# Attention scores computed once, probabilities transposed, value products by features

## The chip, the cores and the metric

The kernel runs on one core of one Trainium2 chip. The metric is the time of one execution in device microseconds (us). The median of three runs of the kernel before is 2375.67 us (2374.99 to 2377.59).

## The reference, cut to what matters

The program is a block of two mixing layers with a feed-forward part; the change touches one of the mixers of the second layer, causal attention over 1024 tokens with 8 heads of 64 features and a forget gate whose running sum `c` is added to the scores:

```
q = rms_norm(q, q_g); k = rms_norm(k, k_g); c = cumsum(log_f)
logits = einsum('bhqd,bhkd->bhqk', q_i, kt) * 64 ** -0.5 + (c_i[:, None] - ck[None, :])
logits = where(kpos <= qpos, logits, -inf)
p = softmax(logits)
o = einsum('bhqk,bhkd->bhqd', p, vt)
```

The output of attention is multiplied by a gate, `silu(z)`, and goes with the other mixers' outputs through an output matrix of 2048 x 1024.

## The kernel before

All data are float32. A product that has to be precise is split: `qs` and `kd` hold a rounded high part, `kl` and the second half of `qs` the remainders, so that two matmuls give the exact score. Heads are treated in pairs hp = 0 to 3 (a pair is 128 features). The program is written as generators ("streams") that `weave` runs in turn, and a scheduler then fixes the order of each engine's instructions; a stream waits for buffers by `need` and for another stream's result by `after`. The stage of attention is made of these streams:

`att_load` (L2225) loads a pair's queries and keys by token, transposes them on PE (`pqk`), and builds, for each head x, `qs` (features in rows 64x to 64x+63, the remainder in the other 64 rows), `qm` (a copy of the high part in rows 0 to 63, zeros below), `kd` (the keys' high part twice) and `kl` (the keys' remainder in rows 0 to 63, and eight rows of -1).

`att_max` (L2282) computes the scores by query rows, block by block (12 blocks of up to 512 columns for a head: `kd` against `qs`, `kl` against `qm`, and a mask on the diagonal). One DVE instruction for each block adds the forget term and takes the row maximum (L2305). When all eight row blocks are done, the maxima are transposed and written into rows 64 to 71 of `qm` (L2315), where they meet the rows of -1 in `kl`.

`att_head` (L2321) waits for that and computes the scores again, this time by key rows (`pT`, L2351 and L2352, another 12 blocks), so that the maximum is subtracted on the way. ACT takes the exponential from PSUM to SBUF (L2355, `pt`), and `pt` is the stationary operand of the value products (L2335): 128 queries by 96 columns of `va`, which has 65 columns for each head, the last of them ones, so that the sum of a row comes with its output. The outputs are divided by it on DVE (L2366, L2367).

`att_out` (L2373) transposes the outputs of a pair back to features, multiplies them by the gate and stores them. `mix_loads` and `final` then read the stored mixer outputs and the output weights; `final` starts when all four pairs are stored, and takes all eight PSUM banks.

Two heads run side by side ("m" and "M", "h" and "H" in `STREAMS2`), and `project2`'s last gates (`pz`) are still computed on PE when the first pair begins. DMA issues are mostly on SyncE (SP), in one queue.

Of the kernel before, what the change touches and what calls it, by code (L numbers as in the profile page):

```python
# [30 lines left out]
STREAMS2 = "sknpl013mM2hH564fx7"  # L31
# [44 lines left out]
def tile_block(ctx: ExitStack, tc: tile.TileContext, A, out):  # L76
# [650 lines left out]
    vau = []  # L727
# [1269 lines left out]
    v_dram = dr.tile([SEQ, 520], F32, name="vd")  # L1997
# [4 lines left out]
    def qkv(q):  # L2002
        yield from after(f"u{q}")
        for j in range(3):
# [10 lines left out]
            if j == 2:  # L2015
                for t in range(4):
                    r0 = (4 * q + t) * 128
                    x = yield from spare("vst", (128, 8, 65), order=("ub", "u"))
                    g.memset(x[:, :, 64:65], 1.0)
                    s.activation(x[:, :, 0:64], p[t][:].rearrange("p (h d) -> p h d", d=64), AF.Copy)  # L2020
                    nc.scalar.dma_start(v_dram[r0:r0 + 128, :], x[:].rearrange("p h d -> p (h d)"))
                    free(x, p[t])
# [202 lines left out]
    def att_load(hp):  # L2225
        if hp == 0:
            yield from after("lru", "sn1")
        yield from need(u=8, ub=2)
        va = ub("vau")
        g.memset(va[:, 1040:1072], 0.0)  # L2230
        nc.sync.dma_start(va[:, 0:1040].rearrange("p (c f) -> p c f", c=8),
                          v_dram[:].rearrange("(c p) f -> p c f", p=128)[:, :, hp * 130:hp * 130 + 130])
        oat = ub("oat", (128, 8, 128))
        for x in range(2):
            heads[2 * hp + x] = dict(qs=u("qs", dt=F32R), qm=u("qm", dt=F32R), kd=u("kd", dt=F32R),
                                     kl=u("kl", dt=F32R), va=va, oat=oat)
            H = heads[2 * hp + x]
# [15 lines left out]
        for hf in range(2):  # L2253
            for j in range(2):
# [9 lines left out]
                for x in range(2):  # L2264
# [3 lines left out]
                    if j == 0:  # L2268
# [13 lines left out]
    def att_max(h):  # L2282
        yield from after(f"pair{h // 2}")
        H = heads[h]
        qs, qm, kd, kl = (H[n] for n in ("qs", "qm", "kd", "kl"))
# [5 lines left out]
        for ib in range(8):  # L2291
            tk = slice(ib * 128, (ib + 1) * 128)
            n = (ib + 1) * 128
            for j0 in range(0, n, 512):
                w = min(512, n - j0)
                yield from need(ps=1, f=1)
                p = bank("pS2")
                diag = j0 + w == n
                wc = max(w, 256)
                pe.matmul(p[:, 0:wc], qs[:, tk], kd[:, j0:j0 + wc], start=True, stop=False)  # L2300
                pe.matmul(p[:, 0:wc], qm[:, tk], kl[:, j0:j0 + wc], start=False, stop=not diag)
                if diag:
                    pe.matmul(p[:, w - 128:w], identb[:], mask[1][:], start=False, stop=True)
                junk = f512("junk")
                v.tensor_tensor_reduce(junk[:, 0:w], p[:, 0:w], nb[:, j0:j0 + w], 1.0, -3e38, op0=ALU.add,  # L2305
                                       op1=ALU.max, accum_out=mx[:, j0 // 512, ib:ib + 1])
                free(p, junk)
                yield 0.45, 0.0
        free(nb)
        v.tensor_tensor(mx[:, 0], mx[:, 0], mx[:, 1], op=ALU.max)  # L2310
        yield 0.0, 2.0
        yield from need(ps=1)
        p = bank("pmr")
        pe.transpose(p[0:8, 0:128], mx[:, 0, :], ident[:])
        v.tensor_tensor(qm[64:72].rearrange("p (c t) -> p c t", c=8), p[0:8, 0:128].unsqueeze(1).to_broadcast([8, 8, 128]),  # L2315
                        ident[0:8, 0:8].unsqueeze(2).to_broadcast([8, 8, 128]), op=ALU.mult)
        free(p)
        done.add(f"max{h}")
        yield 0.1, 1.5

    def att_head(h):  # L2321
        yield from after(f"max{h}")
        H = heads[h]
        qs, qm, kd, kl = (H[n] for n in ("qs", "qm", "kd", "kl"))
        for hf in range(2):
            nj = 4 * (hf + 1)
            yield from need(ps=1)
            pO = bank("pO", (128, 4, 96))
            pe.matmul(pO[:], onesb[:], zerob[:, 0:96].unsqueeze(1).to_broadcast([128, 4, 96]),
                      start=True, stop=False)  # L2330

            def values_(jb, x):
                for b in range(max(0, jb - 4 * hf), 4):
                    o = 130 * jb + 65 * (h % 2)
                    pe.matmul(pO[:, b, :], x[:, jb % 2, b * 128:(b + 1) * 128], H["va"][:, o:o + 96],  # L2335
                              start=False, stop=jb == nj - 1 and b == 3)
                if jb % 2:
                    free(x)

            prev = None  # L2340
            for jb in range(nj):
                i0 = max(0, jb * 128 - hf * 512)
                tk = slice(jb * 128, (jb + 1) * 128)
                if jb % 2 == 0:
                    pt = yield from spare("pt", (128, 2, 512), order=("u", "ub"))
# [253 lines left out]
```

## Time and profile before

| | |
|---|---|
| median of 3 runs | 2375.67 us |
| the profiled execution | 2377.7 us, its span 2376.0 us |
| TensorE (PE) busy | 2240.9 us (94%) |
| VectorE (DVE) busy | 1196.1 us (50%) |
| ScalarE (ACT) busy | 794.1 us (33%) |
| GpSimd (POOL) busy | 941.3 us (40%) |
| stage of attention | 1986.6 to 2189.0 us of the span |

PE's durations are those of a pipeline: one matmul begins before the last has ended, so the rate of PE is read from the distances of starts. Weight loads (PEld) run beside matmuls. A matmul of plain float32 operands is issued as two instructions; one of rounded operands, and a transpose, as one.

### The profile page before, as it was taken

How to read it: one execution, taken by the hardware profiler on the slowest of the kernel's cores; microseconds unless marked ns; L12 is line 12 of the kernel's file. 1: busy time of each engine (PE TensorE's matmuls, PEld its weight loads, DVE VectorE, ACT ScalarE, POOL GpSimd, SP SyncE). 2: the span in 40 equal slices, each digit the busy share in tenths (PEclk: the TensorE clock that was granted, in tenths of full speed). 3: DMA queues.
4: the chain of work that ended last, by engine and by line, in shares of the span. 5: the costliest groups of instructions: out<-in, count | busy, mean ns of one | idle time of the engine just before them, and what ended most of it. 6: DMA issues, size and time to landing. Idle time of an engine off the chain costs nothing.

```text
span 2376.0 us, 29812 instructions
## 1 busy us (share of the span) xinstructions
PE 2240.9 (94%) x11022; PEld 1782.9 (75%) x11022; DVE 1196.1 (50%) x2120; ACT 794.1 (33%) x1417; POOL 941.3 (40%) x846
## 2 busy tenths in 40 slices
PE   5998889797999999999999998999999999999998
PEld 2787657575678888888888876787777777778877
DVE  7689744886871212121121686665545675662011
ACT  2423222433342121111112255343333354543322
POOL 4465534747553222232324534123653133120543
PEclk7999989799999999999999999999999999999999
DMA  7211444344222111111121244243575434231564
GB/s 272 96 48 54 139 151 151 120 150 142 84 82 70 45 49 43 56 49 47 42 62 62 93 142 154 74 155 109 167 211 165 169 111 138 67 116 65 156 192 142
DMA packets 161202, 263.82 MB, mean 111 GB/s; under 512 B 16216, under 2 KB 67224, under 8 KB 161056
## 3 DMA queue, kind: packets, MB, share of 16 engines
q1 hardware_dynamic: 126672, 217.12, 29.0%
q10 hardware_dynamic: 32112, 37.02, 4.7%
q0 software_dynamic: 2272, 7.77, 0.9%
q8 instruction: 87, 1.43, 0.3%
q14 instruction: 59, 0.48, 0.1%
HBM read 208.06 MB, written 52.74 MB: 110 GB/s over the span
## 4 chain that ended last, share of the span: by engine, by line
PE 64%; DVE 16%; DMA 7%; issue 4%; POOL 4%; ACT 3%; SPq 1%; ACTq 0%; POOLq 0%; DVEq 0%
PE pf L253 6%; PE pf L255 6%; PE pf L251 6%; PE pz L251 5%; PE pz L253 5%; PE pz L255 5%; PE pg L238 3%; PE pg L239 3%; PE pg L240 3%; PE pO L2335 2%; DVE cv L809 2%; PE pfo L238 2%; PE pfo L239 2%; PE pfo L240 2%; POOL wlo L212 1%
## 5 line engine op out<-in xcount | busy, mean ns | idle before, releaser
L212 POOL TENSOR_TENSOR wlo<-raw,whi 128x512 fp32r<-128x512 f32 (+1 forms) x285 | 397.7, 1397 | 847.0 <-ACT whi L215 828.2
L215 ACT ACTIVATE whi<-raw 128x512 fp32r<-128x512 f32 (+1 forms) x432 | 267.2, 622 | 984.7 <-PE pf L253 291.7
L212 DVE TENSOR_TENSOR wlo<-raw,whi 128x512 fp32r<-128x512 f32 (+1 forms) x147 | 111.6, 759 | 368.3 <-ACT whi L215 367.8
L255 PE MATMUL pf<-h,wlo 128*128 128x512 f32 x704 | 231.8, 392 | 2.8 <-DVE wlo L212 1.9
L251 PE MATMUL pf<-h,whi 128*128 128x512 f32 x704 | 231.9, 392 | 0.1
L253 PE MATMUL pf<-h,whi 128*128 128x512 f32 x704 | 231.8, 392 | 0.0
L251 PE MATMUL pz<-u,whi 128*128 128x512 f32 x512 | 171.9, 403 | 0.9 <-DVE sptmp L1794 0.6
L253 PE MATMUL pz<-u,whi 128*128 128x512 f32 x512 | 167.6, 395 | 0.0
L255 PE MATMUL pz<-u,wlo 128*128 128x512 f32 x512 | 167.5, 395 | 0.0
L255 PEld LDWEIGHTS pf<-h,wlo 128*128 128x128 f32 x704 | 132.3, 188 | 33.2 <-DVE wlo L212 2.4
L251 PEld LDWEIGHTS pf<-h,whi 128*128 128x128 f32 x704 | 132.5, 188 | 29.6 <-ACT whi L215 0.5
L253 PEld LDWEIGHTS pf<-h,whi 128*128 128x128 f32 x704 | 132.5, 188 | 29.4
L239 PE MATMUL pg<-wlo,act 128*128 128x512 f32 x352 | 138.3, 393 | 0.7 <-DVE wlo L212 0.6
L238 PE MATMUL pg<-whi,act 128*128 128x512 f32 x352 | 137.2, 393 | 1.4 <-ACT whi L215 1.4
L240 PE MATMUL pg<-whi,act 128*128 128x512 f32 x352 | 137.0, 392 | 0.0
L251 PEld LDWEIGHTS pz<-u,whi 128*128 128x128 f32 x512 | 95.9, 188 | 25.2 <-issue 2.6
L253 PEld LDWEIGHTS pz<-u,whi 128*128 128x128 f32 x512 | 96.3, 188 | 22.8 <-issue 1.4
L255 PEld LDWEIGHTS pz<-u,wlo 128*128 128x128 f32 x512 | 95.9, 188 | 22.4 <-issue 1.2
L1579 DVE TENSOR_TENSOR x<-x,pg 128x512 f32<-128x512 f32 x80 | 53.6, 685 | 109.1 <-PE pg L240 108.9
L239 PE MATMUL pfo<-wlo,mix 128*128 128x512 f32 x256 | 100.4, 393 | 1.0 <-POOL wlo L212 0.9
L240 PE MATMUL pfo<-whi,mix 128*128 128x512 f32 x256 | 100.2, 393 | 0.0
L1552 DVE TENSOR_TENSOR a<-a,pf 128x512 f32<-128x512 f32 x44 | 28.6, 683 | 141.0 <-PE pf L255 140.9
(638 smaller groups left out, 4902.3 us busy)
## 6 DMA issues: line engine op xcount, KB each, us to landing
raw<-in_w_ffn_in_dram SPq DMA_DIRECT2D x108, 256.0 KB
wm<-in_w_mod_dram SPq DMA_DIRECT2D x48, 512.0 KB
raw<-in_w_out_dram SPq DMA_DIRECT2D x96, 256.0 KB
raw<-in_w2f_dram SPq DMA_DIRECT2D x66, 256.0 KB
raw<-in_w_ffn_out_dram SPq DMA_DIRECT2D x56, 256.0 KB
raw<-in_w2q_dram SPq DMA_DIRECT2D x48, 256.0 KB
raw<-in_w_in_dram SPq DMA_DIRECT2D x36, 256.0 KB
mraw<-y2d SPq DMA_DIRECT2D x32, 256.0 KB
```

Source lines behind the costliest of these rows:

```text
L212: (v if dve else g).tensor_tensor(lo, full, hi, op=ALU.subtract)
L215: s.activation(hi, full, AF.Copy)
L238: pe.matmul(p, lh, rh, start=start, stop=False)
L239: pe.matmul(p, lh, rl, start=False, stop=False)
L240: pe.matmul(p, ll, rh, start=False, stop=stop)
L251: pe.matmul(p, wh, xh[k], start=k == 0, stop=False)
L253: pe.matmul(p, wh, xl[k], start=False, stop=False)
L255: pe.matmul(p, wl, xh[k], start=False, stop=k == kt - 1)
L809: v.scalar_tensor_tensor(a3, *tap(k), a3, op0=ALU.mult, op1=ALU.add)
L1552: v.tensor_tensor(a_[:], a_[:], pair[1][hf][:], op=ALU.mult)
L1579: v.tensor_tensor(x, x, p[t][:], op=ALU.add)
L2335: pe.matmul(pO[:, b, :], x[:, jb % 2, b * 128:(b + 1) * 128], H["va"][:, o:o + 96], start=False, stop=jb == nj - 1 and b == 3)
```

## The change

The scores are computed once, by query rows (`att_rows`). The DVE instruction keeps the sums of scores and forget term in SBUF (`pr`) as it takes the maximum; `anm` is the negated maximum of a row block, and ACT takes the exponential of a whole row block in place, from SBUF to SBUF, and adds it up in the same instruction (`ell`). PE transposes the probabilities, 128 x 128 at a time, into PSUM, from where DVE and ACT in turn copy them to `pt`. In the value products (`att_values`) 64 columns of `va` are now the stationary operand and the transposed probabilities the moving one, 128 columns; the two heads of a pair write the two halves of the partitions of `pO`, so that the output comes by features and isn't transposed. The gate is multiplied in from `pO`; the reciprocal sums of a pair are transposed (`plr`), written to DRAM, read back spread over partitions (`rb`), and multiplied in by POOL. A head's rows may run two row blocks ahead of its values, and a pair's rows begin when the values of six row blocks of the pair before are written out.

`kl` now holds the keys' remainder in the rows in which `qs` holds the queries' high part, and zeros in the others, so that `qs` serves for both score matmuls; `qm` is gone, and with it the rows for the maxima. `va` has 64 columns for each head. There are three streams in place of four, and values stand ahead of rows in `STREAMS2`.

```diff
-STREAMS2 = "sknpl013mM2hH564fx7"
+STREAMS2 = "sknpl013hmM2564fx7"
...
-                    x = yield from spare("vst", (128, 8, 65), order=("ub", "u"))
-                    g.memset(x[:, :, 64:65], 1.0)
-                    s.activation(x[:, :, 0:64], p[t][:].rearrange("p (h d) -> p h d", d=64), AF.Copy)
+                    x = yield from spare("vst", (128, 512), order=("ub", "u"))
+                    s.activation(x[:], p[t][:], AF.Copy)
...
-        yield from need(u=8, ub=2)
+        if hp > 1:
+            yield from after(f"val{hp - 2}")
+        yield from need(u=8, ub=1)
...
-            g.memset(_r(H["kl"][64:128, :]), 0.0)
-            g.memset(_r(H["kl"][64:72, :]), -1.0)
-            g.memset(_r(H["qm"][64:128, :]), 0.0)
+            g.memset(_r(heads[2 * hp + x]["kl"][64 - 64 * x:128 - 64 * x, :]), 0.0)
...
-                        g.tensor_copy(half(H["qm"], hf)[0:64], _r(half(H["qs"], hf)[r0]))
...
-                        v.scalar_tensor_tensor(half(H["kl"], hf)[0:64], src, col("kg")[r0],
+                        v.scalar_tensor_tensor(half(H["kl"], hf)[r0], src, col("kg")[r0],
...
+    def att_rows(h):
...
+        for ib in range(9):
+            if ib < 8:
+                while ib - ahead.get(hp, 0) > 1 or hp and ahead.get(hp - 1, 0) < 6:
+                    yield 0.0, 0.7
...
+                    pe.matmul(p[:, 0:wc], qs[:, tk], kd[:, j0:j0 + wc], start=True, stop=False)
+                    pe.matmul(p[:, 0:wc], qs[:, tk], kl[:, j0:j0 + wc], start=False, stop=not diag)
+                    if diag:
+                        pe.matmul(p[:, w - 128:w], identb[:], mask[1][:], start=False, stop=True)
+                    v.tensor_tensor_reduce(x[:, j0:j0 + w], p[:, 0:w], nb[:, j0:j0 + w], 1.0, -3e38, op0=ALU.add,
+                                           op1=ALU.max, accum_out=mx[:, j0 // 512, ib:ib + 1])
...
+                nm = small("anm", [128, 1], bufs=4)
+                v.tensor_scalar(nm[:], mx[:, 0, ib:ib + 1], mx[:, 1, ib:ib + 1], -1.0, op0=ALU.max, op1=ALU.mult)
+                s.activation(x[:, 0:n], x[:, 0:n], AF.Exp, bias=nm[:], accum_out=ell[:, hp % 2, h % 2, ib:ib + 1])
...
+                for b0 in range(0, m, 4):
+                    k = min(4, m - b0)
+                    yield from need(ps=1)
+                    p = bank("pP", (128, 4, 128))
+                    for b in range(k):
+                        pe.transpose(p[:, b, :], y[:, (b0 + b) * 128:(b0 + b + 1) * 128], ident[:])
+                    if (m + h) % 2:
+                        s.activation(t[:, b0:b0 + k, :], p[:, 0:k, :], AF.Copy)
+                    else:
+                        v.tensor_copy(t[:, b0:b0 + k, :], p[:, 0:k, :])
...
+    def att_values(hp):
...
+                for jb in range(ib + 1):
+                    for x in range(2):
+                        pe.matmul(pO[64 * x:64 * x + 64, b, :], va[:, jb, 64 * x:64 * x + 64], PT[2 * hp + x, ib][:, jb, :],
+                                  start=jb == 0, stop=jb == ib)
+                free([PT.pop((2 * hp + x, ib)) for x in range(2)])
+                ahead[hp] = ib + 1
...
+            v.scalar_tensor_tensor(zh, zh, 0.5, pO[:].rearrange("p a b -> p (a b)"), op0=ALU.mult, op1=ALU.mult)
...
+        v.reciprocal(le, le)
...
+        pe.transpose(p[0:16, 0:128], le, ident[:])
...
+        v.tensor_copy(lr[:], p[0:16, 0:128])
...
+        nc.sync.dma_start(la_dram[16 * hp:16 * hp + 16, :], lr[:])
...
+            nc.sync.dma_start(rb[64 * x:64 * x + 64], la_dram[16 * hp + 8 * x:16 * hp + 8 * x + 8, :].unsqueeze(0)
+                              .to_broadcast([64, 8, 128]))
...
+        g.tensor_tensor(z[:], z[:], rb[:].rearrange("p a b -> p (a b)"), op=ALU.mult)
```

What stands on PE before, while heads of the first pairs are computed for the second time (`pT` are scores by key rows, `pO` opens a bank by a product with zeros and then takes value products):

```order
L2351 MATMUL pT<-qs,kd 128x256
L2352 MATMUL pT<-qm,kl 128x256
L2354 LDWEIGHTS identb
L2354 MATMUL pT<-mask_81,identb 128x128
L2329 LDWEIGHTS onesb
L2329 MATMUL pO<-zerob,onesb 128x384
L2335 MATMUL pO<-vau,pt 128x96
L2351 MATMUL pT<-qs,kd 128x512
L2352 MATMUL pT<-qm,kl 128x512
L2335 MATMUL pO<-vau,pt 128x96 x6
```

Now PE has, at the end of the first pair (`pP` are transposes of `pr`, `pt_16155` and `pt_16184` the transposed probabilities of its two heads, `pS2_16255` scores of the second pair):

```order
L2359 MATMUL pO_16058<-pt_16184,vau_15505 64x128
L2326 MATMUL pP_16197<-ident_69,pr_16142 128x128 x4
L2326 MATMUL pP_16203<-ident_69,pr_16142 128x128 x4
L2359 MATMUL pO_16058<-pt_16155,vau_15505 64x128
L2359 MATMUL pO_16058<-pt_16184,vau_15505 64x128
L2305 MATMUL pS2_16255<-kd_15855,qs_15854 128x256
L2306 MATMUL pS2_16255<-kl_15856,qs_15854 128x256
L2308 LDWEIGHTS identb_73
L2308 MATMUL pS2_16255<-mask1_86,identb_73 128x128
L2373 MATMUL plr_16260<-ident_69,ell_737 16x128
```

The second pass of scores and the opening of banks are gone; transposes stand among value products, which come head by head in turn, and the next pair's scores begin before the last values of this one.

On DVE before, at the end of the first heads' maxima (`amx` the maxima, `qm` where they are written, `ard` and `oat` the division of outputs):

```order
L2305 ISA amx 128x1
L2310 TENSOR_TENSOR amx<-amx 128x8
L2270 SCALAR_TENSOR_TENSOR qs<-pqk,qg,qs 64x512 x3
L2315 TENSOR_TENSOR qm<-pmr,ident 8x1024
L2270 SCALAR_TENSOR_TENSOR qs<-pqk,qg,qs 64x512
L2366 RECIPROCAL ard<-pO 128x4
L2276 SCALAR_TENSOR_TENSOR kl<-pqk,cols,kd 64x512
L2367 TENSOR_TENSOR oat<-pO,ard 128x4x64
```

Now DVE has, late in the first pair (in brackets the engines for which an instruction waits; ISA is the reduction and the read of its accumulator):

```order
L2330 COPY pt<-pP 128x512 [waits PE_49]
L2309 ISA pr,amx<-pS_16087,negcb 128x384 [waits PE_49]
L2309 ISA amx 128x1
L2314 TENSOR_SCALAR anm<-amx 128x1 [waits DVE_49,Activation_49]
L2314 TENSOR_SCALAR anm<-amx 128x1 [waits DVE_49]
L2365 SCALAR_TENSOR_TENSOR za<-za,pO 128x512 [waits DMAHW3_49,PE_49]
L2309 ISA pr,amx<-pS_16130,negcb 128x512 [waits PE_49]
```

The write of all maxima and the divisions are gone; copies of transposed probabilities and a negation for each row block stand among the reductions, and some negations wait for ACT.

## Rows read from the trace of the kernel before

**Rows 1.** The page's first part: busy time, share, instructions of PE.

```profile
PE 2240.9 (94%) x11022; PEld 1782.9 (75%) x11022; DVE 1196.1 (50%) x2120; ACT 794.1 (33%) x1417; POOL 941.3 (40%) x846
```

**Rows 2.** Stretches: length, busy PE, PEld, DVE, ACT, POOL (instructions), clock, DMA share, GB/s.

```profile
2020.00:2060.00 40.00, 37.04 (x236) 27.99 (x234) 36.31 (x101) 23.03 (x37) 5.91 (x13) 1.00 0.29 86
2060.00:2100.00 40.00, 40.00 (x317) 36.37 (x316) 7.82 (x19) 20.12 (x37) 6.89 (x9) 1.00 0.20 60
2100.00:2140.00 40.00, 36.95 (x235) 28.11 (x235) 34.23 (x107) 16.66 (x27) 8.88 (x8) 1.00 0.37 126
2140.00:2189.00 49.00, 49.00 (x380) 44.52 (x379) 9.14 (x30) 21.83 (x42) 1.27 (x1) 1.00 0.18 55
sum 202.40, PE 193.80 PEld 161.52 DVE 101.84 ACT 94.93 POOL 38.78; mean PE 32.30 PEld 26.92 DVE 16.97 ACT 15.82 POOL 6.46
```

**Rows 3.** The chain of waits from 1986.6 to 2189 us, shares by line.

```profile
by line: PE pO L2335 29.1%; PE pT L2351 8.9%; PE pT L2352 8.2%; DVE junk L2305 6.2%; PE pS L2300 5.4%; PE pS L2301 4.6%; PE pz L251 3.9%; PE pz L253 3.8%; PE pz L255 3.8%; issue 2.8%; DVE qs L2270 2.2%; DVE kl L2276 2.1%; PE pT L2354 2.1%; 
```

**Rows 4.** PE in order of time, 2176 to 2182 us: start, us, what.

```profile
2176.59 3.09 PE L2335 MATMUL pO<-vau,pt 128*128 128x96 f32 x26
2179.47 0.48 PE L2351 MATMUL pT<-qs,kd 128*128 128x512 f32 x1
...
2180.70 0.39 PE L2351 MATMUL pT<-qs,kd 128*128 128x512 f32 x1
2180.93 0.39 PE L2352 MATMUL pT<-qm,kl 128*128 128x512 f32 x1
```

**Rows 5.** PE in order of time around a state-space value product, and its tile.

```profile
1698.93 1.28 PE L1953 MATMUL pyo<-xc,state 128*128 128x128 f32 x10
1700.14 1.97 PE L1966 MATMUL pyd<-lt,xdt 128*64 128x128 f32 x32
1702.04 1.98 PE L1978 MATMUL pst<-xdec,xst 128*128 128x512 f32 x4
...
L1966 PE MATMUL pyd<-lt,xdt x32: 272/273/323, 1700.1 to 1701.8; 128*64 128x128 f32 x32
```

**Rows 6.** PE in order of time, transposes of outputs.

```profile
2187.69 0.93 PE L2384 MATMUL pao<-ident,oat 128*128 128x128 f32 x7
...
2188.46 0.36 PE L2335 MATMUL pO<-vau,pt 128*128 128x96 f32 x2
```

**Rows 7.** Groups on DVE, 1986 to 2189 us: shapes, count, busy us, mean ns, idle.

```profile
L2305 DVE CUSTOM_DVE_ANT_0 junk<-pS,negcb 128x512 f32<-128x512 f32 x48 | 32.0, 686 | 5.1 <-PE pS L2301 2.4 <-DMA za<-zg 1.6 <-DMA negcb<-negcd 0.6
...
L2315 DVE TENSOR_TENSOR qm<-pmr,ident 8x1024 fp32r<-8x1024 f32 x8 | 9.7, 1216 | 4.1 <-PE pmr L2314 4.0
...
L2305 DVE DVE_READ_ACCUMULATOR2_ANT amx<- 128x1 f32 x96 | 7.9, 82 | 0.0
...
L2367 DVE TENSOR_TENSOR oat<-pO,ard 128x256 f32<-128x256 f32 x15 | 6.3, 423 | 0.4
...
L2305 DVE CUSTOM_DVE_ANT_0 junk<-pS,negcb 128x128 f32<-128x128 f32 x16 | 4.6, 287 | 10.7 <-PE pS L2303 10.7
```

**Rows 8.** ACT groups: the first of 1985 to 2200 us, others of the span.

```profile
L2355 ACT ACTIVATE pt<-pT,negc 128x512 f32<-128x512 f32 (+3 forms) x96 | 51.4, 580 | 65.7 <-PE pT L2354 49.0 <-PE pT L2352 12.7 <-DVE amx L2305 1.5
...
L1862 ACT ACTIVATE xst<-ptt 128x512 f32<-128x512 f32 x20 | 11.1, 597 | 4.0 <-PE ptt L1861 4.0
...
L2355 ACT ACTIVATE pt<-pT,negc 128x128 f32<-128x128 f32 x16 | 5.9, 366 | 14.6 <-PE pT L2354 14.5
...
L2112 ACT ACTIVATE ga<-tr,lrun 128x1024 f32<-128x1024 f32 x4 | 5.0, 1248 | 0.1
...
L1659 ACT ACTIVATION_READ_ACCUMULATOR xu<-x 128x1 f32 x8 | 1.5, 184 | 0.0
```

**Rows 9.** Groups on DVE, whole span: a small operation, a PSUM copy.

```profile
L286 DVE TENSOR_SCALAR rs<-rs 128x2 f32<-128x2 f32 x8 | 3.7, 465 | 0.1
...
L455 DVE COPY modrow<-pmod 128x512 f32<-128x512 f32 x4 | 2.7, 686 | 4.5 <-PE pmod L442 4.5
```

**Rows 10.** The chain of waits, 2300 to 2376 us: start, us, what.

```profile
2314.09 3.06 DMA mraw<-y2d
```

More of the change, by code (lines that the diff above doesn't have):

```diff
@@ L2280, in att_load @@
         done.add(f"pair{hp}")
-    def att_max(h):
-        yield from after(f"pair{h // 2}")
+    PT, ahead = {}, {}
+    la_dram = dr.tile([64, 128], F32, name="lad")
+    ell = const.tile([128, 2, 2, 8], F32, name="ell")
+    def att_rows(h):
+        hp = h // 2
+        yield from after(f"pair{hp}")
         H = heads[h]
-        qs, qm, kd, kl = (H[n] for n in ("qs", "qm", "kd", "kl"))
+        qs, kd, kl = (H[n] for n in ("qs", "kd", "kl"))
         nb = yield from spare("negcb", order=("ub", "u"))
@@ L2290, in att_max @@
         yield 0.0, 3.0
[L2291 to L2308, printed above, removed]
@@ L2317, in att_max @@
         free(p)
[L2318 to L2345, printed above, removed]
-                yield from need(ps=1)
-                p = bank("pT")
-                ic = min(i0, 256)
-                i_ = slice(hf * 512 + ic, hf * 512 + 512)
-                diag = jb >= 4 * hf
-                pe.matmul(p[:, ic:512], kd[:, tk], qs[:, i_], start=True, stop=False)
-                pe.matmul(p[:, ic:512], kl[:, tk], qm[:, i_], start=False, stop=not diag)
-                if diag:
-                    pe.matmul(p[:, i0:i0 + 128], identb[:], mask[0][:], start=False, stop=True)
-                s.activation(pt[:, jb % 2, i0:512], p[:, i0:512], AF.Exp, bias=negc[:, h, jb:jb + 1])
-                free(p)
-                yield 0.45, 0.0
-                if prev:
-                    values_(*prev)
-                    yield 0.22 * (4 - max(0, jb - 1 - 4 * hf)), 0.0
-                prev = jb, pt
-            yield 0.0, 1.0
-            values_(*prev)
-            yield 0.22, 0.5
-            rd = small("ard", [128, 4, 1], bufs=4)
-            v.reciprocal(rd[:], pO[:, :, 64:65])
-            v.tensor_tensor(H["oat"][:, 4 * hf:4 * hf + 4, 64 * (h % 2):64 * (h % 2) + 64], pO[:, :, 0:64],
-                            rd[:].to_broadcast([128, 4, 64]), op=ALU.mult)
-            free(pO)
-        free(qs, qm, kd, kl)
-        done.add(f"head{h}")
@@ L2373, in att_out @@
-    def att_out(hp):
-        yield from after(f"head{2 * hp}", f"head{2 * hp + 1}", f"za{hp}")
-        yield from need(u=1)
-        z = u("za")
-        nc.sync.dma_start(z[:], z_dram[f"za{hp}"][:])
-        oat = heads[2 * hp]["oat"]
-        yield 0.0, 3.0
-        for hf in range(2):
-            yield from need(ps=1)
-            p = bank("pao")
-            for c in range(4):
-                pe.transpose(p[:, c * 128:(c + 1) * 128], oat[:, 4 * hf + c, :], ident[:])
-            v.scalar_tensor_tensor(half(z, hf), half(z, hf), 0.5, p[:], op0=ALU.mult, op1=ALU.mult)
-            free(p)
-            yield 0.5, 0.0
-        free(oat, heads[2 * hp]["va"])
+        nc.sync.dma_start(la_dram[16 * hp:16 * hp + 16, :], lr[:])
```

87 lines of the change are left out of this document (68 added, 19 removed).

## Prediction

> **What bounds the kernel now.** I read the page's busy shares first: TensorE (PE) is busy 94% of the span, VectorE (DVE) 50%, ScalarE (ACT) 33% [rows 1]. A share over the whole span says nothing of one stage, so I then asked for a table by stretch of the stage that the change touches, from the first transposes of queries and keys (1986.6 us) to the last value product (2189 us), 202.4 us [rows 2]. The reader is to see two kinds of stretch there. From 2060 to 2100 and from 2140 on PE is busy all the time and DVE has 8 to 9 us of work: these are the score blocks that are computed a second time and the value products. From 2020 to 2060 and from 2100 to 2140 DVE is busy 36.3 and 34.2 us of 40 while PE is at 37: there the row maxima are taken and the next pairs' queries and keys made. The chain of waits over the stage [rows 3] says the same by line: value products 29.1%, the repeated scores (L2351, L2352) 17%, and only about 10% on DVE's lines shown. So PE bounds this stage, and DVE is a close second in a third of it. What follows the stage is 768 output matmuls at 0.23 us each, 177 of the 187 us left; the change does not touch them, so what the stage gains should reach the end.
>
> PE durations on the page overlap, so I take the distance of starts. 26 value products take 2.88 us, 0.111 us each, and a score matmul of 512 columns takes 0.23 us [rows 4]; for 384, 256 and 128 columns I estimate in proportion. A 128x128 transpose takes 0.110 us (seven in 0.77 us) [rows 6].
>
> **The change, part by part.** PE before, at these rates: 576 value instructions (288 products, each issued twice) x 0.111 = 63.9 us; scores, for each head 12 blocks of two matmuls (six of 512 columns, two of 384, four of 256: 4.4 us) and 8 masks at 0.06, 4.9 us, so 39.2 us for eight heads, and that twice, 78.4; 64 transposes of queries and keys 7.0; 32 of outputs 3.5; bank openings and transposed maxima, by the same proportion, about 3.5; the last 96 projection matmuls 22.1. Sum 178 us, in a stage of 202.4: 88%, the rest is waiting and change of operands.
>
> *Scores once.* 39.2 us of PE go, with 96 exponentials on ACT (51.4 us [rows 8]). *The stacked queries instead of a copy.* The low part of the keys meets the same stationary tile as the high part, so no PE work changes; the copies to qm (POOL), two of three clearings and the 1.2 us write of the maxima into qm go (9.7 us of DVE, [rows 7]), and with that write the wait of a head's scores for all its maxima.
>
> *Probabilities transposed.* 288 transposes at 0.110 add 31.7 us to PE. Their 96 evacuations are shared: 48 on DVE, priced by a 512-column PSUM copy of 0.686 and by the 128-column reduction of 0.287 [rows 7, 9], mean size 384 columns, 0.55 us, 26.5 us; 48 on ACT, from 0.597 for 512 columns [rows 8] to about half of that for 128 (an estimate), mean 0.49 us, 23.5 us.
>
> *Value products by features.* The new form, 64 stationary and 128 moving columns with the two heads of a pair in the two column halves, stands in the trace: 32 instructions (16 products) start between 1700.14 and 1701.8, and the next matmul at 1702.04 [rows 5]. Eight pairs take 1.75 us, 0.218 for two products; the old form takes 4 x 0.111 = 0.444. In the new order 131 pairs stand together and 26 products alone; if one alone costs as much as a pair, 157 x 0.218 = 34.2 us in place of 63.9. Going into this form and out again costs something: ten matmuls from 1698.93 at 0.111 would end at 1700.04, the first of the new form comes 0.10 later, and the exit (1701.8 + 0.11 against 1702.04) costs about 0.1 again. The order has 52 visits, so I add 0.2 x 52 = 10.4 us; if the switch is hidden behind a wait, nothing. The Trainium skill, page "TensorEngine Tiling (Array Packing)", section "Key Properties", says that a change of tiling mode drains TensorE, which speaks against small visits; the two gaps above agree. Without the drain the PE sum would be 10 us smaller. No row shows pairs that accumulate over several key blocks; that is a rival below.
>
> PE after: 39.2 + 7.0 + 31.7 + 34.2 + 10.4 + 22.1 = 144.6 us, 33 less. The 96 projection matmuls run while DVE and ACT make the first pair; for each of the four pairs PE has (144.6 - 22.1) / 4 = 30.6 us.
>
> *Exponentials by rows.* 64 on ACT, of 128 to 1024 columns, 0.366 to 1.25 us (the ends are L2355's shortest form and ga's [rows 8]), mean 0.81, 51.7 us, and 64 accumulator reads at 0.184, 11.8 us. 64 negated maxima on DVE: between an accumulator read of 0.082 [rows 7] and a small tensor-scalar of 0.465 [rows 9]; I take 0.2, near the smaller operation, 12.8 us (5 to 30).
>
> DVE in the stage: 101.8 [rows 2] - 9.7 (qm) - 6.3 (oat) + 26.5 + 12.8 = 125 us; without projection and weight work (7 us) 29.6 a pair. ACT: 94.9 - 51.4 + 51.7 + 11.8 + 23.5 = 130.5; without the same other work (12 us) 29.6 a pair. So the three engines come to 30.6, 29.6 and 29.6 us a pair. PE no longer bounds alone: a row block goes from PE (scores) to DVE (maximum), ACT (exponential), PE (transposes), DVE or ACT (copy) and PE (values), and each engine keeps its own order.
>
> How much of the time can three such engines be busy? The rows give one measure: where DVE and PE were both needed, DVE was busy 36.3 of 40 and 34.2 of 40 us, 88% [rows 2]. With a third engine in the loop I take 80%: 30.6 / 0.8 = 38 us a pair (34.8 at 88%; 45 at 68%, which is what a pair takes now: (202.4 - 22.4) / 4). The stage becomes 22 + 4 x 38 = 174 us, 28 less.
>
> *New queueing.* SyncE (SP) now issues, for each pair, a store of the reciprocal sums, two broadcast loads that wait for it, and a store that waits for POOL's product of values and reciprocals. Behind them stand loads of the next pair and of output weights. A trip is about 3 us [rows 10], so at the end some 9 us pass (two trips, the product, the store) before the next weights start; four weight tiles stand ahead of them in the new order, 48 matmuls x 0.23 = 11 us, and that hides it. Uncovered it costs up to 9 us, once. In the pairs before, it is hidden by half a pair of other work. The 65th column of ones, its clearing and va's padding cost nothing on PE.
>
> **The rivals.**
> 1. *Good overlap.* 88% holds with three engines: 22 + 4 x 34.8 = 161, 41 us less: 2335. For it: with the maxima no longer awaited, the new order already brings the next pair's scores between the last value products. At PE's bare sum, 144.6, the gain would be 58 us: 2318; that is the floor.
> 2. *The pairs do not run together* when they accumulate into one bank: 288 products cost 63.9 again, PE has 38 us a pair, at 88% 43.2: stage 195, 2368. Against it: rows 5 differ from the new form in nothing but the accumulation.
> 3. *Slower: the chain of one row block lies open.* The negated maximum lives in four rotating buffers, so DVE waits in its queue until ACT has done the exponential four before it; behind it stand the reductions that free PSUM banks, and PE's next scores wait for those. One block's chain after its scores: reduction about 0.95 with its read, negation 0.2, exponential 1.0, copy 0.5 us and transposes 0.5: 3.2 us, for 32 blocks 101 us. Were 75% of it open, the stage would be 144.6 + 76 = 221, 18 us more: 2394. It decides from 57% on (58 us). Against it: two heads run side by side, and the order puts several score blocks ahead.
> 4. *Nothing moves* although PE's sum falls, 68% overlap: 2375.
>
> That the work isn't taken out is excluded by the order: 192 score matmuls of the second pass are gone.
>
> **How the numbers follow.** The profiled execution took 2377.7 us, its span 2376.0, the median of the runs is 2375.67; I subtract from the median. Forecast: 2375.67 - 28 = 2348 us, chance 58% (own range 2340 to 2360). Rival 1: 16%. Rival 2: 8%. Rival 3: 11%. Rival 4: 7%. The range that leaves out the floor of rival 1 and all of rival 3: 2326 to 2373. A measurement of this kernel tells 0.2%, 4.8 us, from no change. Faster by more: 58 + 16 + 6 (most of rival 2) = 80%; within: 7 + 2 = 9%; slower: 11%.
>
> **What would show it.** In the profile of the changed kernel: the stage about 174 us long, with DVE and ACT busy 70% or more in it and no 40 us stretch where PE is full and DVE at 8; value instructions starting in twos, 0.218 us for two products; transposes 0.110 apart; ACT's accumulator reads near 0.18 and the negations near 0.2; the output matmuls starting about 2161 and lasting 187 us as before. I am wrong if PE waits for DVE at scores or for ACT at transposes for more than 35 us in the stage, if the value instructions start 0.11 apart, or if weights are late after the last pair.

## The result and the profile after

The changed kernel takes 2353.31 us (median of four runs, 2348.66 to 2355.39), the kernel before beside it 2376.63 us: a ratio of 0.9897, 95% interval 0.9878 to 0.9917. The same kernel timed once more in a later group (e9 below) gave 2349.04 us and 0.9881 (0.9862 to 0.9899). The forecast was 2348, the range 2326 to 2373. By both intervals the kernel is faster by 0.8 to 1.4%, well over the 0.2% that was set as the bound.

The profiled execution of after has a span of 2349.8 us against 2376.0. In the page's first line PE has lost 32 us and kept its share; DVE and ACT have gained a little [rows 1]:

```profile
PE 2209.2 (94%) x11002; PEld 1743.7 (74%) x11002; DVE 1209.7 (51%) x2192; ACT 815.1 (35%) x1497; POOL 926.2 (39%) x806
```

The stage now reaches from 1984.2 us (first transposes of queries and keys) to 2165.4 (end of the last value product), 181 us in place of 202.4; the first output matmul starts at 2161.1, before the last values. This is the table by stretch of the stage (length, busy PE, PEld, DVE, ACT, POOL with their instructions, granted clock, DMA share, GB/s):

```profile
2020.00:2040.00 20.00, 17.28 (x118) 12.24 (x119) 16.69 (x49) 16.43 (x33) 0.95 (x1) 0.91 0.28 86
...
2060.00:2080.00 20.00, 17.40 (x107) 12.50 (x109) 15.30 (x50) 13.53 (x28) 2.92 (x3) 0.85 0.26 75
2080.00:2100.00 20.00, 19.43 (x203) 15.55 (x199) 13.27 (x41) 12.93 (x30) 4.66 (x4) 1.00 0.31 101
2100.00:2120.00 20.00, 16.71 (x128) 11.64 (x128) 16.59 (x50) 18.02 (x37) 6.45 (x5) 1.00 0.49 156
...
2140.00:2166.00 26.00, 26.00 (x234) 20.08 (x233) 14.70 (x44) 13.69 (x28) 2.58 (x2) 1.00 0.17 56
```

The reader is to see that the two kinds of stretch of [rows 2], 40 us with DVE at 36 and 40 us with DVE at 8, are gone: from 2020 us on DVE and ACT now have 11 to 18 us of work in every 20. What is new stands in the clock column: 0.91 and 0.85 where the stage before had 1.00.

Two forecasts on PE can be read straight from its own rows in order of time (start, us, what; the step from one row's start to the next gives the time that a row really takes, since durations overlap):

```profile
2080.62 1.97 PE L2326 MATMUL pP<-ident,pr 128*128 128x128 f32 x16
2082.52 1.09 PE L2359 MATMUL pO<-pt,vau 128*64 128x128 f32 x16
2083.54 0.87 PE L2326 MATMUL pP<-ident,pr 128*128 128x128 f32 x6
...
2086.07 0.36 PE L2305 MATMUL pS<-kd,qs 128*128 128x256 f32 x1
2086.27 0.28 PE L2306 MATMUL pS<-kl,qs 128*128 128x256 f32 x1
2086.39 0.23 PE L2308 MATMUL pS<-mask,identb 128*128 128x128 bf16 x1
...
2087.40 1.52 PE L2359 MATMUL pO<-pt,vau 128*64 128x128 f32 x22
2088.86 0.55 PE L2326 MATMUL pP<-ident,pr 128*128 128x128 f32 x3
```

Sixteen transposes take 1.90 us, 0.119 each with the way into the next form; 22 value instructions (eleven products) take 1.46 us with the way out, so the halves of a pair do run together when they accumulate. And the first matmul of a score block, 256 columns, takes 0.20 us behind a transpose, the second 0.12: part of that difference is a term that the prediction missed (next section).

The groups on DVE and ACT in the stage (line, engine, shape, count, busy us, mean ns, idle before and its cause) [rows 7, 8]:

```profile
L2330 DVE COPY pt<-pP 128x512 f32<-128x512 f32 x24 | 16.1, 684 | 1.4 <-PE pP L2326 1.3
L2314 DVE TENSOR_SCALAR anm<-amx 128x1 f32<-128x1 f32 x64 | 13.0, 207 | 1.5 <-ACT pr L2315 0.5
```

```profile
L2328 ACT ACTIVATE pt<-pP 128x512 f32<-128x512 f32 x24 | 14.0, 592 | 12.0 <-PE pP L2326 11.9
L2315 ACT ACTIVATION_READ_ACCUMULATOR pr<-pr,anm 128x1 f32 x64 | 12.1, 189 | 0.0
...
L2315 ACT ACTIVATE pr<-pr,anm 128x1024 f32<-128x1024 f32 x8 | 9.2, 1145 | 1.2 <-DVE anm L2314 1.1
```

Where PE still waits, by the table of its waits over the stage (us in total, times, longest):

```profile
PE pqk L2253 <- DMA qkraw<-qkd: 7.1, 3, 4.6
PE pP L2326 <- ACT pr L2315: 3.8, 5, 1.4
```

The longest, 4.6 us, shows where a step of the prediction failed. SyncE's own rows in order of time and, below them, a line of the DMA view of 2055 to 2063 us (packets, MB, share of the 16 engines) show how it comes about:

```profile
2050.62 0.32 SPq L2377 DMA_DIRECT2D lad<-alr  x1
2054.26 1.11 SPq L2381 DMA_DIRECT2D rb<-lad  x2
2055.46 0.54 SPq L2231 DMA_DIRECT2D vau<-vd  x1
2056.09 3.25 SPq L2240 DMA_DIRECT2D qkraw<-qkd  x3
```

```profile
q1 hardware_dynamic: 2807, 1.95, 91.9%
```

The store of the first pair's reciprocal sums goes out at 2050.62; the broadcast loads behind it wait for it until 2054.26; then come the values of the third pair (512 KB) and its queries and keys (256 KB each). Within 8 us 1.95 MB move and the 16 DMA engines are 91.9% busy; the first queries land at 2061.97, 5.9 us after their issue, where a quiet load of the same size took 3.06 [rows 10]. PE stands still from 2057.4 to 2062.0, its granted clock falls while it stands (0.51 from 2059 to 2062), and it goes on at the lower clock (0.51 from 2062 to 2066, 1.00 from there):

```profile
2062.02 1.12 PE L2253 MATMUL pqk<-ident,qkraw 128*128 128x128 f32 x4 [4.63 <-DMA qkraw<-qkd]
2062.78 0.78 PE L2305 MATMUL pS<-kd,qs 128*128 128x512 f32 x1
2063.36 0.63 PE L2306 MATMUL pS<-kl,qs 128*128 128x512 f32 x1
2063.78 0.41 PE L2305 MATMUL pS<-kd,qs 128*128 128x256 f32 x1
```

The second score matmul of 512 columns takes 0.42 us here, against 0.23 at [rows 4]: 1.2 in place of 2.4 GHz. Of the 20 us with a mean of 0.85, then, PE had work at the lower clock for 4, which cost it some 2. The changed kernel's second profile (e9 below) has the same wait, 4.3 us.

### The profile page after: what moved, and what is told of

The parts are those of the page before. It is cut to its first block, busy times and chain, and to the rows that moved or that the text cites. A ratio compares the mean times of both kernels' runs of the same rounds, so it can differ in the third digit from the quotient of the medians.

```text
span 2349.8 us, 29871 instructions
## 1 busy us (share of the span) xinstructions
PE 2209.2 (94%) x11002; PEld 1743.7 (74%) x11002; DVE 1209.7 (51%) x2192; ACT 815.1 (35%) x1497; POOL 926.2 (39%) x806
## 4 chain that ended last, share of the span: by engine, by line
PE 66%; DVE 15%; DMA 7%; issue 4%; ACT 4%; POOL 4%; SPq 1%; ACTq 0%; POOLq 0%; DVEq 0%
PE pf L253 6%; PE pf L251 6%; PE pf L255 6%; PE pz L251 6%; PE pz L253 6%; PE pz L255 6%; PE pg L238 3%; PE pg L239 3%; PE pg L240 3%; PE pfo L238 2%; PE pfo L239 2%; PE pfo L240 2%; PE pO L2359 2%; DVE cv L809 1%; POOL wlo L212 1%
## 5 line engine op out<-in xcount | busy, mean ns | idle before, releaser
L255 PE MATMUL pz<-u,wlo 128*128 128x512 f32 x512 | 165.8, 395 | 0.0
```

The source lines that it names most:

```text
L255: pe.matmul(p, wl, xh[k], start=False, stop=k == kt - 1)
```

## Where the 26 us came from

The three pieces of the span: the stage starts 2.4 us earlier (1984.2 for 1986.6), is 21.0 us shorter (181.4 for 202.4), and what follows it is 2.6 us shorter (184.4 for 187.0), because ten output matmuls now run inside it. The first piece is not counted as the change's: in the experiments below whose edits touch only work from here on (all but e4) the start lies anywhere from 1981.7 to 1988.6.

For the stage I took, for every matmul, the distance from its start to the next one's start, put the part in which PE stood idle into a row of its own, and summed by tile. In us:

| TensorE's time in the stage | before, by the prediction's rates | before, in the trace | after, forecast | after, in the trace |
|---|---|---|---|---|
| second pass of scores (pT) | 39.2 | 46.9 | 0 | 0 |
| first pass of scores (pS) | 39.2 | 49.4 | 39.2 | 54.4 |
| value products (pO) | 63.9 and 3 for openings | 63.4 | 44.6 | 42.4 |
| transposes of probabilities (pP) | 0 | 0 | 31.7 | 35.0 |
| queries and keys, projections | 29.1 | 30.1 | 29.1 | 31.0 |
| outputs, maxima or sums | 4.0 | 3.3 | 0 | 0.5 |
| output matmuls moved in | 0 | 0 | 0 | 2.5 |
| sum | 178 | 193.1 | 144.6 | 165.8 |
| idle | 24 | 8.6 | 29 | 15.3 |

So before, PE was not 88% but 96% occupied, and the second pass of scores was worth 46.9 us, not 39.2. After, the sum is 27.3 us lower (forecast 33), and idle time 6.7 us higher.

Why a score pass costs more than its rate shows in [rows 4] once one looks at the neighbours. PE before, at 2064 us, and its operand loads (PEld) at the same place:

```profile
2064.49 0.47 PE L2351 MATMUL pT<-qs,kd 128*128 128x512 f32 x1
2064.80 0.39 PE L2352 MATMUL pT<-qm,kl 128*128 128x512 f32 x1
2065.03 0.23 PE L2354 MATMUL pT<-mask,identb 128*128 128x128 bf16 x1
2065.07 0.48 PE L2351 MATMUL pT<-qs,kd 128*128 128x512 f32 x1
```

```profile
2064.46 0.19 PEld L2351 LDWEIGHTS pT<-qs,kd 128*128 128x128 f32 x1
2064.57 0.19 PEld L2352 LDWEIGHTS pT<-qm,kl 128*128 128x128 f32 x1
...
2065.03 0.20 PEld L2351 LDWEIGHTS pT<-qs,kd 128*128 128x128 f32 x1
```

The second matmul's load starts 0.23 us ahead of it, under the first matmul, and it takes 0.23 us. The first one's load starts 0.03 or 0.04 us ahead, and the matmul takes 0.31. It is not its place in the block that decides, but what runs before it. The 0.23 of [rows 4] is itself read from the first matmul of a block, the one at 2180.70, which stands directly behind another score matmul, and its load starts 0.22 us ahead:

```profile
2180.48 0.19 PEld L2351 LDWEIGHTS pT<-qs,kd 128*128 128x128 f32 x1
```

In the whole repeated pass 73 of 96 blocks begin behind an instruction of another kind (a mask, a value product, the opening of a bank, a transpose), and their first matmul takes 0.09 us more than the rate on average; the other 23 begin behind a score matmul and keep the rate. The prediction took the 0.23 of [rows 4] for all.

Part of these 0.09 us is a matter of booking. By the distance of starts a value product of the kernel before that stands ahead of a score matmul gets 0.057 us in place of its 0.111, and a transpose 0.028 in place of 0.109. The two rows together cost 0.03 us more than their rates behind such a value product, 0.06 behind a mask, and nothing behind a transpose. So some 2 us of the 46.9 are time of the value products (43 such places), and the row "value products" is as much too low.

That the late load is the cause fits these rows and e1 below, but no run took it away alone. (The Trainium skill, page "TensorE: Matmul & The Clock Gate", section "The mechanism", says in one sentence that a load overlaps a running matmul only when they lie in different row groups, and in another that a load into a background weight buffer is pulled ahead as well. Here the load at 2064.57 runs under a matmul with all 128 rows: the measurement goes against the first sentence; the second no run here tests.)

## The experiments

The order of each engine is settled by the builder, so every edit of this stage also moves rows that it does not name. The changed kernel itself gave 2353.3 and 2349.0 us in two groups; differences of 4 us and less are not read, unless both kernels ran in one group.

**e1, scores computed twice.** The repetition stands ahead of the block's own two matmuls:

```
+ pe.matmul(p[:, 0:wc], qs[:, tk], kd[:, j0:j0 + wc], start=True, stop=False)
+ pe.matmul(p[:, 0:wc], qs[:, tk], kl[:, j0:j0 + wc], start=False, stop=True)
  pe.matmul(p[:, 0:wc], qs[:, tk], kd[:, j0:j0 + wc], start=True, stop=False)
```

> Each score block is computed twice into the same bank (96 blocks, 192 more matmuls, 39.2 us of TensorE at the rates of the kernel before; the second time overwrites the first, the result does not change). Everything else stays, though the engines' order is rebuilt around it. Theory (TensorE's work still sets the stage, beside some 30 us of waits): the stage of 181 us grows by most of the 39 us, at least by 25: 2378 to 2392 us. Rival (the loop of scores, maximum, exponential, transpose and copy sets the stage, and TensorE has slack in it): less than 10 us more, below 2363 us.

Measured: 2371.61 us (2366.62 to 2376.44), ratio 0.998 (0.9969 to 0.9991): 18 us more than after, between theory and rival. The PE rows of one block show the price of a repetition:

```profile
2085.69 0.44 PE L2305 MATMUL pS<-kd,qs 128*128 128x384 f32 x1
2085.97 0.34 PE L2306 MATMUL pS<-kl,qs 128*128 128x384 f32 x1
2086.15 0.34 PE L2307 MATMUL pS<-kd,qs 128*128 128x384 f32 x1
2086.32 0.34 PE L2308 MATMUL pS<-kl,qs 128*128 128x384 f32 x1
2086.50 0.23 PE L2310 MATMUL pS<-mask,identb 128*128 128x128 bf16 x1
```

The whole stage as one stretch (columns as above):

```profile
1986.40:2187.00 200.60, 195.19 (x1482) 154.50 (x1480) 121.40 (x359) 117.92 (x245) 28.67 (x25) 0.99 0.30 95
```

The first matmul, behind a value product, takes 0.28, the other three 0.17 to 0.18: the extra cost belongs to the matmul that follows another kind of instruction, and a repetition inside the block is cheaper than a pass of its own. By the same sums as above, scores grow from 54.4 to 85.9 us, 31.5, while idle time falls from 15.3 to 5.4 and the clock of the stage rises from 0.96 to 0.99. So about 10 of 31 us went into TensorE's pauses: there is slack, but no more than the pauses that the trace shows.

**e2, the halves of a pair apart.**

```
- for jb in range(ib + 1):
-     for x in range(2):
+ for x in range(2):
+     for jb in range(ib + 1):
```

> The value products run head by head: all key blocks of one head, then all of the other, so that no two neighbours lie in different column halves. The same instructions in number and size. Theory: the gain on value products is that two of different halves run at once; apart, 288 products of two instructions of 0.109 us cost 63 us in place of 31 to 34, and most of 29 us reaches the end: 2373 to 2383 us, with 16 products in about 3.5 us in place of 1.9. Rival (the smaller products are cheap by themselves): 16 products still in about 1.9 us and 2353 us. Rival (TensorE has slack): products slow, time below 2362 us.

Measured: 2370.29 us (2368.32 to 2375.47), ratio 0.9968 (0.9958 to 0.9978), 17 us more than after; the theory had 20 to 30. The chain of waits has 16 products (32 instructions) of both kernels, first with the pairs apart:

```profile
2055.98 3.26 PE pO L2359 x32
```

and in the changed kernel:

```profile
2051.35 1.90 PE pO L2359 x32
```

1.36 us less for 16 products of 288. The sum over value products is 64.6 us apart and 42.4 together, a difference of 22 us, of which 17 reach the end. Of the change's gain, 17 us hang on the order of two loops.

**e10, transposes twice.**

```
- for b in range(k):
+ for b in [*range(k)] * 2:
```

> Each of the 288 transposes of probabilities is issued twice into the same place (31 us more of TensorE, the result does not change). It prices what the change added there. From the two experiments that added work to TensorE (39 us gave 18, 22 us gave 17) I expect half to three quarters at the end: 2369 to 2377 us. If the transposes lie in TensorE's waits for VectorE and ScalarE: below 2362 us.

Measured: 2377.95 us (2375.18 to 2383.91), ratio 1.0008 (0.9997 to 1.0019), 29 us more than e9 on the same chip. TensorE's time on transposes rises by 31.5 us (35.0 to 66.5), and idle time falls by 3 only. A second set of transposes is paid almost in full, more than I expected: it hides in no wait. Together e1, e2 and e10 say that added TensorE work comes through at 0.6 to 0.9; TensorE is still the bound, with some 10 us of pauses.

**e3, ten buffers for the negated maximum.**

```
- nm = small("anm", [128, 1], bufs=4)
+ nm = small("anm", [128, 1], bufs=10)
```

> The negated maximum gets ten rotating buffers in place of four. If VectorE's wait for the exponential four before it held the loop (the slower rival of the prediction), 8 us or more go: 2345 us or less. Theory: that wait is short, the time stays within 4 us of 2353 (the order is rebuilt by the builder, which moves a few us either way).

Measured: 2357.55 us (2355.05 to 2359.24), ratio 0.9916 (0.9901 to 0.9931). Nothing is gained; the 4.2 us more are a little over the 4 expected, and are not read. The group of the negations above shows the same: 0.5 us of waiting for ACT in the whole stage. The slower rival's mechanism is not there.

**e8, all copies of transposes on ScalarE.**

```
- if (m + h) % 2:
+ if True:
      s.activation(t[:, b0:b0 + k, :], p[:, 0:k, :], AF.Copy)
```

> All 96 copies of transposed probabilities run on ScalarE (48 more, some 23 us), none on VectorE (some 25 us less): VectorE 94 us and ScalarE 140 us in the stage. If VectorE is what the loop waits for: 2345 us or less. If ScalarE is: 2360 us or more. If neither bounds alone and TensorE's work sets the stage: within 5 us of 2353.

Measured: 2357.39 us (2354.92 to 2361.42), ratio 0.9916 (0.9891 to 0.9941). The whole stage as one stretch (columns as above):

```profile
1988.50:2181.70 193.20, 176.44 (x1319) 133.56 (x1317) 97.41 (x312) 136.49 (x295) 29.89 (x26) 0.95 0.33 102
```

Against 118.5 and 116.6 us in after, VectorE is 21 us lighter, and the time does not fall; ScalarE is 20 us heavier, and the time rises by 4 us, which is not read. The stage itself is longer here, since more of the output matmuls run inside it. VectorE does not bound; that ScalarE does not is shown to within these 4 us.

**e4, the loads of queries and keys first.** They are issued ahead of the wait for the pair two before:

```
+ if hp > 1:
+     while ahead.get(hp - 2, 0) < 7:
+         yield 0.0, 0.7
...
+ yield from need(raw=2)
+ for un in units[:2]:
+     raw_load(*un)
+ if hp > 1:
      yield from after(f"val{hp - 2}")
```

> The first two loads of queries and keys of the third and fourth pair are issued when seven of eight row blocks of the pair two before are done, ahead of its store of reciprocal sums and of the broadcast loads that wait for that store, and ahead of the load of the values. Theory: the wait of 4.6 us for qkraw at 2057 to 2062 goes, and with it part of the slower clock behind it (0.85 from 2060 to 2080, 3 us): 2344 to 2349 us. Rival (this wait is the place where other slack shows, the loop makes it up elsewhere): within 3 us of 2353.

Measured: 2370.88 us (2368.79 to 2372.74), ratio 0.9979 (0.9964 to 0.9994). The edit did more than meant: the first two pairs load early too and so hold two of the three buffers that the weights before this stage share. Ahead of the stage, from 1900 to 1984 us, TensorE is busy 76.9 us in place of 84.0, and the stage starts at 1996.5 in place of 1984.2. Both theory and rival are missed: the run says nothing of the wait in question, but much of the three buffers.

**e5, the same loads from another pool**, for the third and fourth pair alone:

```
+ raws[hf, j] = C["f" if hp > 1 else "raw"].get("qkraw")
...
  if hp > 1:
+     while ahead.get(hp - 2, 0) < 5:
+         yield 0.0, 0.7
+     yield from need(f=2)
+     for un in units[:2]:
+         raw_load(*un)
      yield from after(f"val{hp - 2}")
```

> Of the third and fourth pair the queries and keys are loaded into tiles of another pool (five of 128x512 that stand empty in this stage), no longer into the three that the weights share, and the first two loads are issued when five row blocks of the pair two before are done, ahead of its store of reciprocal sums and its broadcast loads. The first two pairs load as they did. Theory: the wait of TensorE for qkraw at 2057 to 2062 (4.6 us) and the half clock behind it (3 us) go: 2345 to 2350 us. Rival (the loop has no use for the earlier start): within 3 us of 2353.

Measured: 2353.41 us (2348.99 to 2358.74), ratio 0.9904 (0.9877 to 0.993): the rival. The wait at 2057 is gone, and the chain of waits shows what is late next at the same place:

```profile
2054.50 0.46 PE pqk L2261 x4
2054.98 0.57 ACT qs L2271
...
2059.59 0.69 ACT kd L2276
2060.29 0.77 DVE qs L2272
...
2061.32 0.42 DVE kl L2277
```

The transposes of the third pair's queries now run at 2054.5, but making its operands (copies of 0.68 us on ACT, differences of 0.77 on DVE, among the row work) takes until 2062 and later, and PE pauses there, 1.74 us at the longest. The stretches 2060 to 2080 and 2100 to 2120 stand at a granted clock of 0.83. Over the whole stage idle time is 14.7 us (15.3 in after) and the clock 0.93 (0.96): what the wait gave back went into other pauses and the clock. That the whole chain between two pairs counts, and not its first link alone, fits this but is not shown by it.

**e6, sums and broadcasts on GpSimd's queue.**

```
- nc.sync.dma_start(la_dram[16 * hp:16 * hp + 16, :], lr[:])
+ nc.gpsimd.dma_start(la_dram[16 * hp:16 * hp + 16, :], lr[:])
...
- nc.sync.dma_start(rb[64 * x:64 * x + 64], ...)
+ nc.gpsimd.dma_start(rb[64 * x:64 * x + 64], ...)
```

> The store of the reciprocal sums and the two broadcast loads behind it go on GpSimd's queue in place of SyncE's. Theory of the prediction (this queueing is hidden but for nothing): within 3 us of 2353. Rival (SyncE's wait of 3.3 us for the store delays the third pair's loads, which TensorE then waits for): 2345 to 2350 us, and the wait for qkraw shorter by 3 us. Should GpSimd's own queue suffer, its clearing of kl comes late and TensorE waits for kl: above 2356 us.

Measured: 2356.35 us (2352.53 to 2360.14), ratio 0.9915 (0.9891 to 0.9939). The chain of waits from 2050 to 2061 us has this piece:

```profile
2052.50 7.56 DMA qkraw<-qkd
```

The load is issued 3.6 us earlier than in after (2056.09), takes 7.6 us in place of 5.9, and PE still waits 4.45 us. Taking the broadcasts out of the queue did not take the load out of the crowd: they and the values move at the same time. The rival's shorter wait is not there. The third alternative's number was met by 0.35 us, but PE has no wait for `kl` in this trace. By its time, 3 us above after, the run lies at the edge of the theory that the queue costs nothing; but the wait that the queue was to explain is still there, so the run does not price the queue, and what the bytes in flight have to do with the wait was not separated.

**e7, three row blocks in flight; e11, four.**

```
- while ib - ahead.get(hp, 0) > 1 or hp and ahead.get(hp - 1, 0) < 6:
+ while ib - ahead.get(hp, 0) > 2 or hp and ahead.get(hp - 1, 0) < 6:
```

(e11 has 3 there.)

> A head may have three row blocks begun before the value products of the first are done, in place of two. If the chain of one row block (scores, maximum, exponential, transposes, copy: 3 to 4 us) lies open in the loop, more blocks in flight cover it: 8 us or more go, 2345 us or less, and TensorE's short waits at scores fall from about 25 us to under 15. If they come from three engines near their full load and from the DMAs, within 4 us of 2353.

> Four row blocks of a head in flight in place of two (three gave 2349.9 us). If TensorE's short waits at scores come from the length of one block's chain, this covers what three left: 2343 to 2348 us. If three were enough, or buffers run out, 2348 to 2353 us.

Measured: three, 2349.86 us (2342.16 to 2351.24), ratio 0.9881 (0.9855 to 0.9907); four, 2359.06 us (2354.98 to 2363.85), ratio 0.9925 (0.991 to 0.9941). With three the stage's idle time falls from 15.3 to 11.6 us and no wait of PE for qkraw is left, but by its interval the kernel can't be told from after. With four it is slower, against both expectations; a 6 us load of queries stands in its chain at 2057.75, and the clock of 2060 to 2080 is 0.74. Why a fourth block costs this was not separated.

**e9, after once more; e12, three blocks and the loads of e5 together.**

> The changed kernel itself, nothing edited, beside the three others of this group on one chip: 2349 to 2356 us, the ratio to the kernel before 0.989 to 0.991.

> Three row blocks in flight, and queries and keys of the last two pairs loaded early into the empty pool. With three blocks in flight no wait of TensorE for these loads was left in the trace, so the second edit should bring little: 2345 to 2351 us. If the early loads still shorten the way between two pairs: below 2345 us.

Measured on one chip: after 2349.04 us (2347.67 to 2351.11), ratio 0.9881 (0.9862 to 0.9899); e12 2342.76 us (2341.65 to 2346.04), ratio 0.9858 (0.9842 to 0.9875). The ratios' intervals touch, but no run of the one lies among those of the other: e12 is some 6 us faster and beats both kernels. Two of its stretches:

```profile
2040.00:2060.00 20.00, 19.45 (x189) 15.21 (x188) 14.97 (x48) 14.86 (x34) 4.15 (x5) 1.00 0.62 198
2060.00:2080.00 20.00, 18.22 (x138) 13.77 (x139) 16.17 (x54) 15.24 (x34) 2.28 (x4) 1.00 0.14 41
```

and the longest waits of its PE:

```profile
PE pS L2312 <- DVE qs L2272: 2.6, 2, 2.2
PE pqk L2261 <- ACT qs L2271: 2.2, 1, 2.2
```

Neither edit alone could be told from after; together they can. That it takes both is not shown, since e12 and e7 overlap by their intervals (0.9842 to 0.9875 and 0.9855 to 0.9907). What the trace fits is that the third pair's loads come in time and that there are enough row blocks of the second pair to run while its operands are made. The stage is 171 us long, idle 8.3, and from 2040 on the clock is 1.00.

## Why the prediction was right, and where it was not

- **The bound.** Right: TensorE's work set the stage before and sets it still. e1, e2 and e10 add 31, 22 and 31 us to it and cost 18, 17 and 29; taking 21 us from VectorE and giving 20 to ScalarE (e8) gains nothing.
- **Scores once, 39.2 us.** Too small. The pass was worth 46.9 in the trace, mainly because in 73 of 96 blocks the first matmul follows another kind of instruction and takes 0.09 us more than the rate taken from [rows 4]; some 2 us of that belong to the value products before it. The same error sits in the pass that stays (39.2 forecast, 49.4 before, 54.4 after, the last with the lower clock and with the way from masks into value products in it), so much of it cancels in the difference. The sum of 178 us "at its rates" was 15 too low, and where 12% of the stage was read as pauses, TensorE stood idle for 4%.
- **Transposes, 31.7 us.** 35.0; per transpose 0.110 was right inside a run of them (1.90 us for sixteen with the switch behind).
- **Value products, 34.2 and 10.4 for the way in and out.** 42.4 against 44.6. The pairing is there and e2 prices it at 22 us on TensorE; the way out shows as 0.20 us from the last value instruction to the next matmul, where inside a run the steps are about 0.10, and the way in as 0.20 from the last transpose before a visit, where between transposes it is 0.109. There are 50 visits: the 10.4 us for 52 were right. The rival of pairs that do not run together is refuted.
- **Small operations.** The negation was taken at 0.2 us between 0.082 and 0.465, and is 0.207; ScalarE's accumulator read 0.189 for 0.184; the 512-column copies 0.684 and 0.592 for 0.686 and 0.597. VectorE is 119 us busy for 125, ScalarE 117 for 130.5. The exponentials' ends are 0.400 and 1.145 us for 0.366 and 1.25.
- **The overlap, 80%.** The forecast stage was 174 us, the measured one 181; the first output matmul started at 2161.1, as forecast, but ahead of the last values and not behind them. By the prediction's own rates, 144.6 of 181.4 us is 80%, but the reading behind that figure was wrong: it stands for two things, scores that cost more than their rate (no pause at all) and real pauses, 15 us and the lower clock.
- **"In the pairs before, it is hidden by half a pair of other work."** The step that failed by the trace. Between the first and the third pair it was not hidden: PE waited 4.6 us for queries that stood behind the broadcasts and shared the DMA engines with them, and some 2 us went at the lower clock after it. No repair of this place alone paid: e5 removed the wait for the loads and gained nothing, other pauses and the clock taking its place, and e6 left the wait as it was. With another block in flight as well (e12) the kernel is 6 us faster than after, though not clearly faster than with the block alone (e7).
- **At the end of the stage** no weights were late: the output matmuls start before the last value products and last 188.7 us from 2161.1, with other work between the first ten, for 187.
- **The slower rival** (four buffers, an open chain of a block): refuted by e3 and by 0.5 us of waiting in the trace. One more block in flight (e7) took 4 us of TensorE's idle time away, by its times not told from nothing.

The total came out near the forecast partly by luck. For the stage the prediction had 33 us less work and 5 us more idle time, 28 us; the traces have 27 less and 7 more, 21. The second pass gave back 8 us more than its rate said. Against that stand 5 us more on the scores that stay, 3 more on the transposes, 1 each on value products, outputs, and queries and keys, and 2.5 for output matmuls that moved in. The 26 us of the two profiles come from these 21, from the output matmuls that moved, and from a start of the stage 2.4 us earlier that nobody forecast. By the medians it is 23 us in the first group and 27 in that of e9.

## What to carry to other kernels

Take the price of a block, not of its best matmul: step from start to start over two or three whole blocks, since a matmul behind one of another kind was counted a third longer here, and take the row before it into the sum, since part of that is its time. When products with 64 columns come in pairs, alternate the halves instruction by instruction; the order of two loops was 17 us here. And where work goes pair by pair, look at the place between two pairs: loads, operand copies and row work form one chain there, and removing one link (e5) showed nothing, while the same edit with one more block in flight (e12) went with 6 us less.

## What the runs showed of the hardware

- A score matmul of 512 columns takes 0.23 us directly behind another score matmul, its load starting some 0.23 us ahead, and 0.31 to 0.32 behind a mask, a full-width value product or a transpose, its load starting 0.03 to 0.04 ahead (256 columns: 0.12 and 0.20). Summed with the row before it, the extra over the two rates is 0.06 behind a mask, 0.03 behind such a value product and nothing behind a transpose. A repetition within the block has none (0.28, then 0.18, 0.17, 0.18 at 384).
- Leaving the form with 64 columns costs TensorE about 0.1 us, 0.20 to the next matmul where steps inside are about 0.10, and entering it as much, 0.20 from the last transpose where between transposes it is 0.109. The full-width value products of the kernel before have no such step ahead of transposes (0.112, inside 0.111). (The Trainium skill, page "TensorEngine Tiling (Array Packing)", section "Key Properties", speaks of a drain without a price; the rows agree and give one.)
- While TensorE stood for 4.6 us its granted clock fell to the lower level (0.51 from 2059 to 2062 us), and it stayed there until 2066 (a 512-column matmul in 0.42 us); from there it was 1.00. e5 had no pause over 1.8 us in that place and still 0.83 from 2060 to 2080; e12 had none over 0.7 from 2040 on and 1.00.
- A load of 256 KB landed in 5.9 us with the DMA engines 91.9% busy (after), in 7.6 with broadcasts and values in flight (e6), and in 3.06 in a quiet place.
